# Two edits to the second block of a two-block network: the latents' norms summed on TensorE, and the last feed-forward's first four column tiles computed ahead of its norm's factor

## Chip, cores and metric

The kernel runs as one program on one core of a Trainium2 chip. The metric is the device time of one execution in microseconds, as a median over runs. All numbers of the profile come from one profiled execution of the kernel before.

## The reference, cut to what matters

A first block (two transformer layers over 256 tokens of width 1024) makes `h`, whose last step is `rmsnorm(h, final_norm)`. That result is the stream `x` of a second block, which normalises it again, modulates it, mixes it in several branches, and closes with a feed-forward. `D` is 1024, the feed-forward's width is 2816, and tokens are held in a permuted order that changes nothing here.

```
x  = rmsnorm(h, final_norm)                               # end of block one
hn = rmsnorm(x, norm1_g) * (1 + sc1) + sh1                # both factors: the "latents' two norms"
mix = ... dn_inputs, recurrence, branches of hn ...
x  = x + g1 * mix
a, b = split((rmsnorm(x, norm2_g) * (1 + sc2) + sh2) @ w_ffn_in)
x  = x + g2 * ((silu(a) * b) @ w_ffn_out)                 # the last feed-forward
return rmsnorm(x, final_g)
```

With `r` the factor of a token (a number per column of the transposed layout, where features lie on partitions and tokens on the free axis), `(x * gain * r + sh) @ W = r * ((x * gain) @ W) + sh @ W`. The first product needs no `r`, and `sh @ W` is one number per output feature.

## The kernel before

All activations are transposed: `[128 partitions, 8, 256]`, feature on partition and block, token on the free axis. Every large product is exact to float32 by three fp32r matmuls (`mm3`, L276: high weight by high x, high weight by low x, low weight by high x), all issued by `mm` at L274. A unit of weights is a `[128, 1024]` tile; `weights` (L250 to L268) loads it over SP's queue into `wst` (3 buffers), rounds it to `wh` on ScalarE in two halves (L262) and subtracts on VectorE, or on GpSimd while `onpool` is positive, to get `wl` (L263, two halves). `wh` and `wl` have 3 buffers each.

An instruction's place on its engine is not the order of the source: a planner fills each engine's queue in advance from its own costs, taking among the ready instructions the one traced first; `urgent()` moves what it holds some 100 places forward. `behind()` and `lastsq` keep weight rounding on ScalarE behind the last square. Generators run beside a main loop: `beside` and `tick` let a side generator take its next step each time a unit of weights is asked for. PSUM has two pools of 4 banks, `ps` (tiles named bank) and `acc`.

**The latents (L954 to L1006)** are a side generator beside `dn_inputs` of the context's values. `sumsq` (L301 to L324) squares the eight blocks of `h` in four ScalarE instructions of 512 columns (L309) for the first sum, and in eight of 256 columns with `final_norm` as the scale (L313) for the second; VectorE adds the four pairs (L317, L319) and folds them (L323). `col_sums` (L326) sums a `[128, 256]` tile over partitions with the tile as the stationary operand and a column of ones moving, the answer a column per 128 tokens. Four small VectorE instructions (L969 to L972) and the eight of `root` (L348 to L363) turn four columns into factors, `across` (L366, transposes at L370) spreads them over partitions as rows, and ScalarE copies the rows to `lrows` (L980, L981). Then each of the eight blocks takes two VectorE products (L988), a rounding on ScalarE (L911) and a difference on VectorE (L912). The first product of the latents that reads them is `dn_inputs` for q, whose first two units go block by block (`cols_into` with `outer`).

**The last feed-forward (L1650 to L1676)** begins where the product with `w_o` has ended. `gated_residual` (L1631) adds each block to `x2` (L1637), squares it (L1641), and adds five of the squares (L1646); four tiles of squares go to `col_sums`. `modulate` then runs `rsqrt` (L345) and `root`, `across`, and for each block the product with gain and factor (L906), rounding with the shift (L911) and difference (L912). Each `f` of 11 makes two banks `a` and `b` of two column tiles each from four units of `w_fin`; the first `f` goes block by block over two units. ScalarE takes the silu of bank a (L1668), VectorE multiplies by bank b (L1669), `split_pair` (L1410) rounds, and `down` adds the rows' product into `acc` one `f` later. `self.onpool = self.np1` (L1653) gives the first three units' differences to GpSimd.

Of the kernel before, what the change touches and what calls it, by code (L numbers as in the profile page):

```python
# [9 lines left out]
F32 = mybir.dt.float32  # L10
F32R = mybir.dt.float32r
I32 = mybir.dt.int32
AF = mybir.ActivationFunctionType
OP = mybir.AluOpType
AX = mybir.AxisListType

P = 128
T = 256
D = 1024
KD = D // P  # L20
HD = 64
EPS = 1e-6
# [6 lines left out]
NFF = 22  # L29
# [165 lines left out]
def run(g):  # L195
    for _ in g:
        pass
# [33 lines left out]
class Net:  # L231
# [722 lines left out]
    def latent(self):  # L954


        nc = self.nc
        h = self.h
        yield
        gg = self.sm.tile([P, KD], F32, name="lgg", bufs=1)  # L960
        nc.vector.tensor_mul(gg, self.gf, self.gains[:, 0])
        parts = self.lparts
        s1 = self.sumsq(h, parts=parts, eng=nc.gpsimd if 0 else nc.vector)
        s2 = self.sumsq(h, self.gf, parts=parts)
        yield
        with self.urgent():
            cs = self.col_sums((s1, s2))
            v = self.sm.tile([P, 4], F32, name="lv", bufs=1)
            nc.vector.tensor_scalar(v[:, 2:4], cs[:, 0:2], 1.0 / D, EPS, op0=OP.mult, op1=OP.add)  # L969
            nc.vector.tensor_scalar(v[:, 0:2], v[:, 2:4], D * EPS, None, op0=OP.mult)  # L970
            nc.vector.tensor_add(v[:, 0:2], v[:, 0:2], cs[:, 2:4])
            nc.vector.tensor_scalar(v[:, 0:2], v[:, 0:2], 1.0 / D, None, op0=OP.mult)  # L972
            rows = self.across(self.root(v, 4))
        yield
# [9 lines left out]
        for k in range(KD):  # L984
            q = pairs(h[:, k])
            t = self.sm.tile([P, T], F32, name="mt")
# [644 lines left out]
    def gated_residual(self, acc, gate, add):  # L1631
# [15 lines left out]
                ss[0] = s  # L1647
        return ss

    def swiglu(self):  # L1650
        nc = self.nc
        x = []
        self.onpool = self.np1  # L1653
        run(self.modulate(self.x2, self.gains[:, 2], self.mod[:, 3, 0], x, self.ss))
        pend = []

        down = self.downward(self.a["w_fout"], NFF, pend, self.ends)

        for f in range(NFF // 2):
            if f:  # L1660
                self.lastsq = None
            ab = []
            for base in (0, NFF):
                bv = self.bank2()
                self.cols_into(bv, [self.a["w_fin"][base + 2 * f + n] for n in range(2)], x, f == 0 and self.ko & 1)
                ab.append(bv)
            s = self.t2k("sw")
            nc.scalar.activation(s, ab[0], AF.Silu)  # L1668
            nc.vector.tensor_mul(s, s, ab[1])  # L1669
            ah = self.sm.tile([P, 2, T], F32R, name="ah", tag="w2k", bufs=self.nw2k)  # L1670
            al = self.sm.tile([P, 2, T], F32R, name="al", tag="w2k", bufs=self.nw2k)
            self.split_pair((ah, al), 0, s)
            pend.append((ah, al))
            if f:
                down(False)
        self.ss = self.gated_residual(down(True), self.mod[:, 5, 0], nc.gpsimd if self.gadd else nc.vector)  # L1676
# [127 lines left out]
```

## Time and profile before

| What | Value |
|---|---|
| Median of three runs | 1237.73 us |
| The three runs | 1237.47, 1237.73, 1238.69 us |
| Profiled execution, its own time | 1240.33 us |
| Its span in the trace | 1238.5 us |
| TensorE matmul busy | 1183.0 us (96%) |
| VectorE busy | 899.4 us (73%) |
| ScalarE busy | 636.3 us (51%) |
| GpSimd busy | 124.7 us (10%) |

Times in the trace are from the start of the span. PE is TensorE's matmuls, DVE VectorE, ACT ScalarE, POOL GpSimd. A busy PE is not PE at its peak, since matmuls overlap: in a full stream one of 256 columns starts every 0.12 us and is shown as 0.28 us. A float32 matmul shows as two instructions.

### The profile page before, as it was taken

To read this page: it belongs to the slowest core of one execution; us is meant where nothing else is said; L and a number is where in the kernel's file an instruction comes from. 1 tells how busy PE (TensorE), PEld (TensorE's weight loads), DVE (VectorE), ACT (ScalarE), POOL (GpSimd) and SP (SyncE) were. 2 spreads that over 40 slices of the span, in tenths; PEclk is the share of its full clock that TensorE was granted. 3 is DMA by queue.
4 is the path that set the end of the run, shared out by engine and by line. 5 is a ranking of instruction groups with operands and counts; after the bars stand their busy time and mean duration, and the time that the engine had idled before them with its cause. 6 is when DMAs were issued, how large, how long until landed. Compare 5 with 4: busy or idle time off the path is not lost.

```text
span 1238.5 us, 24745 instructions
## 1 busy us (share of the span) xinstructions
PE 1183.0 (96%) x9858; PEld 1122.1 (91%) x9858; DVE 899.4 (73%) x1784; ACT 636.3 (51%) x1247; POOL 124.7 (10%) x213
## 2 busy tenths in 40 slices
PE   8999999999999989999999799997999996999997
PEld 6779999999977889999999788897989996999997
DVE  6998996556988487675657999997665677555555
ACT  5654545555755565644445656543333545444444
POOL 1000000000010000064000310374000002000000
PEclk8999999999999989999999989998999997999998
DMA  6766687555553635457545525776423552655552
GB/s 213 238 208 240 227 291 268 185 187 188 156 174 119 210 120 173 169 171 203 164 144 165 166 83 165 240 272 215 148 81 103 179 179 86 205 187 177 186 184 85
DMA packets 65779, 221.43 MB, mean 179 GB/s; under 512 B 10048, under 2 KB 11456, under 8 KB 65664
## 3 DMA queue, kind: packets, MB, share of 16 engines
q1 hardware_dynamic: 64800, 218.29, 53.3%
q0 software_dynamic: 864, 1.57, 0.7%
q8 instruction: 77, 1.26, 0.4%
q14 instruction: 38, 0.31, 0.1%
HBM read 218.00 MB, written 1.84 MB: 177 GB/s over the span
## 4 chain that ended last, share of the span: by engine, by line
PE 64%; issue 13%; DVE 12%; POOL 6%; DMA 4%; ACT 1%; DVEq 0%; SPq 0%; POOLq 0%; ACTq 0%
PE acc L274 34%; PE bank L274 28%; DVE wl L263 3%; POOL bo L1280 1%; POOL bz L1281 1%; DVE cy L1036 1%; PE bank L565 1%; DVE xl L298 1%; DVE wmst L882 1%; DMA bl<-there 1%; DMA xc<-back 1%; ACT wh L262 1%; POOL bw L1259 1%; DMA wmst<-w_mod 1%; DVE qkT L533 1%
## 5 line engine op out<-in xcount | busy, mean ns | idle before, releaser
L262 ACT ACTIVATE wh<-wst 128x512 fp32r<-128x512 f32 x708 | 411.7, 623 | 436.8 <-PE bank L274 165.4
L263 DVE TENSOR_TENSOR wl<-wst,wh 128x512 fp32r<-128x512 f32 x696 | 464.9, 700 | 216.7 <-ACT wh L262 216.0
L274 PE MATMUL bank<-xh,wh 128*128 128x256 f32 x1024 | 293.9, 287 | 2.0 <-ACT xh L911 1.1
L274 PE MATMUL bank<-xl,wh 128*128 128x256 f32 x1024 | 293.0, 286 | 1.8 <-DVE xl L298 1.8
L274 PE MATMUL bank<-xh,wl 128*128 128x256 f32 x1024 | 292.6, 286 | 1.6 <-DVE wl L263 1.6
L274 PEld LDWEIGHTS bank<-xh,wh 128*128 128x128 f32 x1024 | 198.6, 194 | 3.2 <-ACT xh L911 1.5
L274 PEld LDWEIGHTS bank<-xh,wl 128*128 128x128 f32 x1024 | 198.6, 194 | 2.8 <-DVE wl L263 2.6
L274 PEld LDWEIGHTS bank<-xl,wh 128*128 128x128 f32 x1024 | 198.6, 194 | 2.5 <-DVE xl L298 2.4
L274 PE MATMUL acc<-ah,wh 128*128 128x256 f32 x688 | 192.1, 280 | 0.0
L274 PE MATMUL acc<-al,wh 128*128 128x256 f32 x688 | 191.7, 279 | 0.0
L274 PE MATMUL acc<-ah,wl 128*128 128x256 f32 x688 | 191.6, 279 | 0.0
L274 PE MATMUL acc<-xh,wh 128*128 128x256 f32 x640 | 184.5, 289 | 0.4 <-ACT wh L262 0.4
L274 PE MATMUL acc<-xl,wh 128*128 128x256 f32 x640 | 183.2, 287 | 0.4 <-DVE xl L912 0.4
L274 PE MATMUL acc<-xh,wl 128*128 128x256 f32 x640 | 182.8, 286 | 0.5 <-DVE wl L263 0.4
L274 PEld LDWEIGHTS acc<-ah,wl 128*128 128x128 f32 x688 | 129.2, 188 | 0.1
L274 PEld LDWEIGHTS acc<-ah,wh 128*128 128x128 f32 x688 | 129.1, 188 | 0.0
L274 PEld LDWEIGHTS acc<-al,wh 128*128 128x128 f32 x688 | 128.9, 187 | 0.0
L274 PEld LDWEIGHTS acc<-xh,wh 128*128 128x128 f32 x640 | 124.0, 194 | 2.8 <-issue 1.4
L274 PEld LDWEIGHTS acc<-xl,wh 128*128 128x128 f32 x640 | 123.9, 194 | 2.1 <-issue 1.0
L274 PEld LDWEIGHTS acc<-xh,wl 128*128 128x128 f32 x640 | 123.8, 194 | 1.3 <-DVE wl L263 0.9
L274 PE MATMUL acc<-wl,xh 128*128 128x512 f32 x176 | 70.6, 401 | 2.3 <-DVE wl L263 2.3
L274 PE MATMUL acc<-wh,xh 128*128 128x512 f32 x176 | 70.6, 405 | 1.5 <-ACT wh L262 1.5
(344 smaller groups left out, 1515.8 us busy)
## 6 DMA issues: line engine op xcount, KB each, us to landing
wst<-w_up SPq DMA_DIRECT2D x64, 512.0 KB, 3.6
wst<-w_down SPq DMA_DIRECT2D x64, 512.0 KB, 3.4
wmst<-w_mod SPq DMA_DIRECT2D x48, 512.0 KB, 4.8
wst<-w_fin SPq DMA_DIRECT2D x44, 512.0 KB, 3.3
wst<-w_in SPq DMA_DIRECT2D x39, 512.0 KB, 3.7
wst<-w_mgate SPq DMA_DIRECT2D x24, 512.0 KB, 3.3
wst<-w_fout SPq DMA_DIRECT2D x22, 512.0 KB, 3.3
wst<-w_qkv SPq DMA_DIRECT2D x20, 512.0 KB, 3.4
```

The costliest lines, as they stand in the source:

```text
L262: nc.scalar.activation(wh[:, c:c + n], st[:, c:c + n], AF.Copy)
L263: i = (nc.gpsimd if self.onpool > 0 else nc.vector).tensor_tensor(wl[:, c:c + n], st[:, c:c + n], wh[:, c:c + n].bitcast(F32), op=OP.subtract)
L274: self.nc.tensor.matmul(out, lhsT, rhs, start=start, stop=stop, skip_group_check=skip)
L298: nc.vector.scalar_tensor_tensor(xl[:, k], src, gain, xh[:, k].bitcast(F32), op0=OP.mult, op1=OP.subtract)
L533: nc.vector.tensor_copy(qk[:, :, t * P:(t + 1) * P], bk.rearrange("p (c q) -> p c q", c=4))
L565: nc.tensor.transpose(bk[:, c * P:(c + 1) * P], s[:, g, c * P:(c + 1) * P], self.ident)
L882: nc.vector.scalar_tensor_tensor(pr, st, 1.0, cv[v], op0=OP.mult, op1=OP.mult, accum_out=mod[:, part, v, k:k + 1])
L1036: nc.vector.scalar_tensor_tensor(y4[:, j], pad[:, j, :, tap:tap + CHUNK], w[:, j, tap:tap + 1], y4[:, j], op0=OP.mult, op1=OP.add)
L1259: pool.tensor_tensor(w, A[t][:, a].rearrange("p h (b j) -> p h b j", b=4), m, op=OP.mult)
L1280: pool.tensor_tensor(o, lt[:, c:, j:c].to_broadcast([P, n, c]), Z[:, j:c, 0:c].to_broadcast([P, n, c]), op=OP.mult)
L1281: pool.tensor_tensor(Z[:, c:, 0:c], Z[:, c:, 0:c], o, op=OP.subtract)
```

## The change

The latents' sums go to TensorE: each pair of squared blocks is the stationary operand, and two columns move, one of ones and one of the squares of `final_norm`, so that both sums come of one set of squares. The squares scaled by `final_norm` and VectorE's additions are gone.

In the last feed-forward, `ahead` rounds `x2 * gain` (no factor, no shift) to a pair `U` with two more columns, the shift and zero. `ahead_units` traces the norm's sum and `root`, then the products of `U` with the first two units (tiles 0 and 1 of a), then the row and the modulated pair `x` for all later `f`, then tiles 0 and 1 of b from `U`. Each of the four tiles fills one bank of 258 columns; column 256 is the shift's product, which is copied out and added as ScalarE's bias or in a VectorE product after the row's factor. The line that gave three units' differences to GpSimd is gone.

```diff
--- before.py
+++ after.py
@@ -959,16 +959,24 @@
         yield
         gg = self.sm.tile([P, KD], F32, name="lgg", bufs=1)
         nc.vector.tensor_mul(gg, self.gf, self.gains[:, 0])
-        parts = self.lparts
-        s1 = self.sumsq(h, parts=parts, eng=nc.gpsimd if 0 else nc.vector)
-        s2 = self.sumsq(h, self.gf, parts=parts)
-        yield
+        w2 = self.sm.tile([P, KD, 2], F32, name="lw2", bufs=1)
+        nc.vector.memset(w2[:, :, 0:1], 1.0)
+        nc.vector.tensor_mul(w2[:, :, 1:2], self.gf[:, :, None], self.gf[:, :, None])
+        cs = self.bank()[:, 0:4].rearrange("p (t c) -> p t c", t=2)
+        for j in range(4):
+            sq = self.t2k("sq")
+            nc.scalar.activation(sq, h[:, 2 * j:2 * j + 2], AF.Square)
+            for n in range(2):
+                k = 2 * j + n
+                for t in range(2):
+                    self.mm(cs[:, t], sq[:, n, t * P:(t + 1) * P], w2[:, k], k == 0 and t == 0, k == KD - 1, True)
+            if j == 2:
+                yield
         with self.urgent():
-            cs = self.col_sums((s1, s2))
             v = self.sm.tile([P, 4], F32, name="lv", bufs=1)
-            nc.vector.tensor_scalar(v[:, 2:4], cs[:, 0:2], 1.0 / D, EPS, op0=OP.mult, op1=OP.add)
+            nc.vector.tensor_scalar(v[:, 2:4], cs[:, :, 0], 1.0 / D, EPS, op0=OP.mult, op1=OP.add)
             nc.vector.tensor_scalar(v[:, 0:2], v[:, 2:4], D * EPS, None, op0=OP.mult)
-            nc.vector.tensor_add(v[:, 0:2], v[:, 0:2], cs[:, 2:4])
+            nc.vector.tensor_add(v[:, 0:2], v[:, 0:2], cs[:, :, 1])
             nc.vector.tensor_scalar(v[:, 0:2], v[:, 0:2], 1.0 / D, None, op0=OP.mult)
             rows = self.across(self.root(v, 4))
         yield
@@ -1647,26 +1655,77 @@
                 ss[0] = s
         return ss
 
+    def ahead(self):
+
+
+        nc = self.nc
+        U = [self.act.tile([P, KD, T + 2], F32R, name=n, tag="xs", bufs=4) for n in ("uh", "ul")]
+        sh = self.sm.tile([P, KD, 2], F32, name="ush", bufs=1)
+        nc.vector.memset(sh[:, :, 1:2], 0.0)
+        nc.vector.tensor_copy(sh[:, :, 0:1], self.mod[:, 3, 0][:, :, None])
+        nc.scalar.activation(U[0][:, :, T:], sh, AF.Copy)
+        nc.vector.tensor_sub(U[1][:, :, T:], sh, U[0][:, :, T:].bitcast(F32))
+        for k in range(KD):
+            self.split(self.x2[:, k], k, self.gains[:, 2, k:k + 1], U[0][:, :, 0:T], U[1][:, :, 0:T])
+        self.xs = x = self.pair()
+        return U, x
+
+    def ahead_units(self, U):
+        nc = self.nc
+        r = []
+        steps = self.row_steps(self.x2, r, ss=self.ss)
+        next(steps)
+        next(steps)
+        bv, row = [], None
+        for base in (0, NFF):
+            w = [self.weights(self.a["w_fin"][base + n]) for n in range(2)]
+            bk = [self.bank() for _ in range(2)]
+            for k in range(KD):
+                for n in range(2):
+                    ws = slice(k * P, k * P + P)
+                    self.mm3(bk[n][:, 0:T + 2], (w[n][0][:, ws], w[n][1][:, ws]), (U[0][:, k], U[1][:, k]), k == 0, k == KD - 1)
+            bv += bk
+            if row is None:
+                run(steps)
+                row = self.sm.tile([P, T], F32, name="nrow")
+                nc.scalar.activation(row, r[0], AF.Copy)
+                for k in range(KD):
+                    self.modulated(self.x2, k, self.gains[:, 2], self.mod[:, 3, 0], row, *self.xs)
+        c = self.sm.tile([P, 4], F32, name="usc", bufs=1)
+        s, t = self.t2k("sw"), self.t2k("sq")
+        for i, b in enumerate(bv):
+            n = i % 2
+            nc.vector.tensor_copy(c[:, i:i + 1], b[:, T:T + 1])
+            nc.vector.tensor_mul(t[:, n], b[:, 0:T], row)
+            if i < 2:
+                nc.scalar.activation(s[:, n], t[:, n], AF.Silu, bias=c[:, i:i + 1])
+                if n == 1:
+                    t = self.t2k("sq")
+            else:
+                nc.vector.scalar_tensor_tensor(s[:, n], t[:, n], c[:, i:i + 1], s[:, n], op0=OP.add, op1=OP.mult)
+        return s
+
     def swiglu(self):
         nc = self.nc
-        x = []
-        self.onpool = self.np1
-        run(self.modulate(self.x2, self.gains[:, 2], self.mod[:, 3, 0], x, self.ss))
         pend = []
+        U, x = self.ahead()
 
         down = self.downward(self.a["w_fout"], NFF, pend, self.ends)
 
         for f in range(NFF // 2):
             if f:
                 self.lastsq = None
-            ab = []
-            for base in (0, NFF):
-                bv = self.bank2()
-                self.cols_into(bv, [self.a["w_fin"][base + 2 * f + n] for n in range(2)], x, f == 0 and self.ko & 1)
-                ab.append(bv)
-            s = self.t2k("sw")
-            nc.scalar.activation(s, ab[0], AF.Silu)
-            nc.vector.tensor_mul(s, s, ab[1])
+            if f == 0:
+                s = self.ahead_units(U)
+            else:
+                ab = []
+                for base in (0, NFF):
+                    bv = self.bank2()
+                    self.cols_into(bv, [self.a["w_fin"][base + 2 * f + n] for n in range(2)], x)
+                    ab.append(bv)
+                s = self.t2k("sw")
+                nc.scalar.activation(s, ab[0], AF.Silu)
+                nc.vector.tensor_mul(s, s, ab[1])
             ah = self.sm.tile([P, 2, T], F32R, name="ah", tag="w2k", bufs=self.nw2k)
             al = self.sm.tile([P, 2, T], F32R, name="al", tag="w2k", bufs=self.nw2k)
             self.split_pair((ah, al), 0, s)
```

## Rows read from the trace of the kernel before

**Rows 1.** Page, parts 1 and 5: busy; group, count, busy us, mean ns, idle.

```profile
PE 1183.0 (96%) x9858; PEld 1122.1 (91%) x9858; DVE 899.4 (73%) x1784; ACT 636.3 (51%) x1247; POOL 124.7 (10%) x213
...
L262 ACT ACTIVATE wh<-wst 128x512 fp32r<-128x512 f32 x708 | 411.7, 623 | 436.8 <-PE bank L274 165.4
```

**Rows 2.** TensorE's waits: us in total, times, longest.

```profile
PE bank L370 <- DVE rsy L361: 17.1, 4, 7.6
...
PE bank L274 <- DVE U L1309: 6.7, 1, 6.7
```

**Rows 3.** Windows, latents: length, busy us of PE, PEld, DVE, ACT, POOL, clock, DMA.

```profile
691.00:703.60 12.60, 12.52 (x105) 12.29 (x103) 11.83 (x23) 11.34 (x24) 3.98 (x8) 1.00 0.59 174
703.60:714.50 10.90, 3.19 (x14) 2.14 (x12) 9.08 (x22) 5.01 (x15) 8.74 (x18) 0.71 0.45 146
714.50:718.30 3.80, 3.75 (x17) 3.40 (x18) 3.80 (x10) 2.54 (x7) 1.97 (x4) 0.50 0.00 0
718.30:724.20 5.90, 5.90 (x51) 5.51 (x49) 5.90 (x20) 2.80 (x6) 0.15 (x2) 0.99 0.00 0
...
735.00:760.00 25.00, 24.11 (x249) 21.71 (x248) 24.83 (x55) 9.89 (x20) 1.93 (x6) 1.00 0.47 148
```

**Rows 4.** Groups of VectorE, 691 to 727 us: count, busy us, mean ns, idle.

```profile
L319 DVE TENSOR_TENSOR ssp<-ssp,sq 128x512 f32<-128x512 f32 x4 | 2.7, 685 | 0.0
...
L317 DVE TENSOR_TENSOR ssp<-sq 128x512 f32<-128x512 f32 x2 | 1.4, 682 | 0.0
...
L970 DVE TENSOR_SCALAR lv<-lv 128x2 f32<-128x2 f32 x1 | 1.2, 1221 | 0.0
L323 DVE TENSOR_TENSOR ss<-ssp 128x256 f32<-128x256 f32 x2 | 0.8, 414 | 0.0
```

**Rows 5.** VectorE's timeline, latents: start, us, instruction.

```profile
700.90 0.41 DVE L323 TENSOR_TENSOR ss<-ssp 128x256 f32<-128x256 f32 x1
...
702.66 0.15 DVE L969 TENSOR_SCALAR lv<-bank 128x2 f32<-128x2 f32 x1
...
709.01 1.31 DVE L361 SCALAR_TENSOR_TENSOR rsy<-rst,rsy 128x4 f32<-128x4 f32 x1
```

**Rows 6.** ScalarE's timeline, latents: the scaled squares, first four.

```profile
695.25 1.70 ACT L313 ACTIVATE sq<-h,k_final_norm 128x256 f32<-128x256 f32 x4
```

**Rows 7.** GpSimd's timeline, latents and feed-forward.

```profile
700.99 5.52 POOL L263 TENSOR_TENSOR wl<-wst,wh 128x512 fp32r<-128x512 f32 x4
...
1025.65 7.38 POOL L263 TENSOR_TENSOR wl<-wst,wh 128x512 fp32r<-128x512 f32 x6 [171.35 <-ACT wh L262]
```

**Rows 8.** TensorE's timeline, start of the feed-forward.

```profile
1024.34 1.57 PE L274 MATMUL bank<-ones,sq 128*128 128x1 f32 x12
```

**Rows 9.** Windows of the feed-forward's start, columns as in rows 3.

```profile
1035.20:1039.20 4.00, 3.90 (x18) 3.88 (x19) 3.55 (x9) 2.11 (x6) 0.00 (x0) 0.50 0.13 49
...
1044.50:1050.10 5.60, 5.60 (x46) 5.60 (x47) 1.98 (x4) 3.25 (x6) 0.00 (x0) 1.00 0.47 148
```

**Rows 10.** Groups of VectorE, 1019 to 1050 us, columns as in rows 4.

```profile
L1637 DVE SCALAR_TENSOR_TENSOR x<-acc,hg,x 128x256 f32<-128x256 f32 x8 | 3.6, 476 | 2.5 <-PE acc L274 2.5
L912 DVE SCALAR_TENSOR_TENSOR xl<-mt,mod,xh 128x256 fp32r<-128x256 f32 x8 | 3.5, 483 | 0.7 <-ACT xh L911 0.7
L906 DVE SCALAR_TENSOR_TENSOR mt<-x,gains,bank 128x256 f32<-128x256 f32 x8 | 3.5, 475 | 0.8 <-PE bank L370 0.8
L263 DVE TENSOR_TENSOR wl<-wst,wh 128x512 fp32r<-128x512 f32 x4 | 2.6, 689 | 3.7 <-ACT wh L262 3.7
L1646 DVE TENSOR_TENSOR ss<-ss,sq 128x256 f32<-128x256 f32 x3 | 1.2, 417 | 0.1
L355 DVE TENSOR_TENSOR rst<-rsy 128x2 f32<-128x2 f32 x1 | 1.2, 1193 | 0.0
```

**Rows 11.** VectorE's timeline, the same chain at the end of the kernel.

```profile
1229.81 0.16 DVE L345 TENSOR_SCALAR rsv<-bank 128x2 f32<-128x2 f32 x1 [1.32 <-PE bank L274]
...
1231.38 0.16 DVE L361 SCALAR_TENSOR_TENSOR rsy<-rst,rsy 128x2 f32<-128x2 f32 x1
```

## The prediction

> **What bounds the kernel now.** I read the page first: TensorE's matmuls are busy 1183.0 of 1238.5 us, VectorE 899.4 [rows 1], so the kernel is a nearly full TensorE stream with a few holes, and an edit pays where it closes a hole. TensorE's waits name them: 17.1 us in four waits for the last instruction of `root`, the longest 7.6 us, and one wait of 6.7 us late in the mixer for `U` of the recurrence [rows 2]. Two of the four are where this change works: the latents' norms, and the last feed-forward's norm.
>
> The windows show the first place [rows 3]. From 691 to 703.6 us TensorE (12.52 of 12.60) and VectorE (11.83) are both full. From 703.6 to 714.5 us TensorE works 3.19 of 10.9 us: the context's values are done and the latents are not ready. Its granted clock falls with that idleness, and is 0.50, the lower level of 1.2 GHz, until 718.3 us. VectorE is full again at 714.5 to 718.3 us and at 735 to 760 us (24.83 of 25), so in the mixer it stands close behind TensorE as a bound.
>
> At the second place the sum over partitions ends at 1024.34 + 1.57 = 1025.9 us [rows 8], `root` waits and works until 1033.5 us, and the first 18 matmuls from 1035.2 us run at 0.50 of the clock, 3.9 us for what takes 18 x 0.12 = 2.2 us at full clock; from 1044.5 us the stream is full, and 46 matmuls end the first `f` at 1050.1 us [rows 9]. After that nothing but TensorE counts until the tail.
>
> **Why `root` is slow there.** Its small instructions take 1.19 us [rows 10] while GpSimd subtracts for three units from 1025.65 to 1033.0 us [rows 7]. At the end of the kernel, with GpSimd idle, the same nine take 1229.81 to 1231.54, 1.73 us [rows 11]. In the latents L970 (1.22 us) and L361 (1.31 us) are stretched in the same way [rows 4, 5], inside GpSimd's stretch from 700.99 us on [rows 7].
>
> **The latents, step by step.** Removed from VectorE: 2.7 + 1.4 + 0.8 = 4.9 us by durations [rows 4]; some 0.6 us of that is overlap of neighbouring records, so 4.3; two tiny instructions for the columns are added at about 0.15 each, as L969 [rows 5]. Net 4.0 us. Removed from ScalarE: eight squares, 2 x 1.70 = 3.4 us [rows 6], off the path itself but ahead of the second sum. Added to TensorE: 16 products, two instructions each, against eight removed. Twelve one-column instructions take 1.57 us [rows 8], 0.131 each; a second column is taken as free, since 128 stationary columns are loaded for each. (32 - 8) x 0.131 = 3.1 us more. It falls into the full stretch before 703.6 us and moves the values' end to 706.7 us; what hides it is the hole, which lasts past the end of `root` at 710.3 us [rows 5], and if that hole closes it costs its 3.1 us.
>
> The chain: the last plain square ends by about 695.3 us (the scaled ones follow at 695.25 [rows 6]). Its eight instructions take 1.05 us, with 0.3 us of hand-over L969 starts at 696.7 instead of 702.66 us [rows 5]: 6.0 us earlier. From there the twelve small instructions, the spreading and the eight blocks are the same work. If the chain decides, 6.0 us are won, and up to 1.7 us more from a clock that need not fall (17 matmuls in 3.75 us [rows 3] against 2.0). If VectorE's queue decides, only what is taken off it, 4.0 us. VectorE is full on both sides of the hole, so I lean to it: 5 us. The ends: 7.7 us, and 0 if the mixer is held elsewhere.
>
> **The feed-forward, step by step.** The products of tiles 0 and 1 of a (48 matmuls) no longer need the row. They need `U`, block by block, and the differences of units 0 and 1, which are now VectorE's. From 1025.9 us VectorE has at most: `root` 1.7 us [rows 11], eight differences for `U` at 0.48, 3.9 us, priced as L912, and four halves at 0.69, 2.8 us [rows 10]: 8.4 us, to 1034.3 us. (Part of `U` will be done sooner: before 1025.9 us VectorE has 3.6 us of L1637 and four L1646 at 0.42.) The second unit's first half is the last that block 0 needs, so the stream starts between 1030 and 1033 us; I take 1031.5. TensorE has by then stood nearly still for 5 us, so I take the half clock for 18 matmuls again, 1.7 us: 1031.5 + 5.8 + 1.7 = 1039.0.
>
> Then tiles 0 and 1 of b. Unit 3 can be rounded only when the first units' buffers are free, at the end of that: 0.62 us on ScalarE [rows 1] and 0.69 on VectorE [rows 10], 1.3 us in which TensorE waits as it does now. 1039.0 + 1.3 + 5.8 = 1046.1 us for the first matmul of the next `f`, against 1050.1: 4 us won. VectorE's check: 1034.3 + 3.5 + 3.5 (L906, L912) + 2.8 for units 2 and 3 + 0.6 for reading the first bank (0.15 and 0.48) = 1044.7 us, just under 1046.1. So VectorE is all but the bound, and its queue is where it can go wrong. Ends: 7 us (start at 1030.3, full clock, 1.3 of waiting: 1043.2) and 1.5 us (unit 3's half behind the modulated blocks, near 1041.5, and 5.8 after it, with queueing).
>
> **Small edits.** Two more columns in 96 matmuls are 192 columns, under 0.1 us at the 0.12 us for 256. The shift's four tiny instructions need only the modulation and fit before the stage. Two silu of half the size replace one: at most 0.5 us on ScalarE, which is idle there. The closing of the first `f` grows on VectorE from one product to four columns, four products and two more, some 3.5 us; behind it in VectorE's queue stand the halves of units 4 and 5, and TensorE waits for those. No DMA is added; unit 3's load, on SP's queue behind the release of unit 0's buffer, starts later than now, and unit 3's wait for the end of the first 48 matmuls covers it. If that cover is gone, the load shows in full.
>
> **Sum.** 5 + 4 = 9 us. The profiled execution took 1240.33 us (span 1238.5) and would take 1231.3; it stands 2.6 above the median, so in medians 1237.73 - 9 = **1228.7 us**.
>
> **Rivals.**
> *The mixer is held elsewhere.* For it: VectorE full at 735 to 760 us and a 6.7 us wait behind the recurrence's chain [rows 2, 3]. Against: those chains also begin with the latents. Only the feed-forward counts: 1233.7 us. Chance 0.15.
> *GpSimd gets in the earlier chain's way.* ScalarE has less to do and could round q's units sooner, so GpSimd's four halves move along with the chain. Six of its instructions would take 1.19 instead of 0.16 us, where two do now: 4 x 1.03 = 4.1 us back. 0.9 + 4 = 4.9 us: 1232.8 us. Chance 0.15. The Trainium skill has a rule for it (SBUF — State Buffer, Who interferes with whom): a VectorE instruction with two inputs in SBUF waits out a whole GpSimd instruction that reads SBUF. The stretched rows agree in that they are stretched; L970 has one input and is stretched too [rows 4].
> *VectorE becomes the bound of the feed-forward* (the slower side). All four `ps` banks are held by the first `f`, where two were, so the next `f` waits for VectorE to read one. If its queue runs in series, modulated blocks and both last units first (1034.3 + 7.0 + 2.8 = 1044.1), the products of b end at 1049.9, closing (some 2.9) and unit 4's half (0.7) follow, 1053.5, and the half clock costs 1.7 again: 1055.2, 5 us later than now. With the latents at their low end of 0: 1242.8 us. It decides from the point where the next `f` starts later than 1050.1 us by more than the latents gave. Chance 0.1.
> *The order does not change.* The planner could keep the products behind the row, or spend the gain in another order of the mixer: 1237.7 us. Chance 0.05.
>
> **How the numbers follow.** The forecast has the other 0.55, with 1224.5 to 1232.5 for itself. A measurement here tells 0.2%, 2.5 us, from no change, so faster is under 1235.2. Faster: 0.55 and nearly all of the first two rivals and the edges of others, 0.79; same 0.11; slower 0.10. The range goes up over the first two rivals to the unchanged time, 1238, and down to both terms at their upper ends, 1237.7 - 14.7 = 1223, with 2 us for planner order: 1221.
>
> **What would show it.** Right: no wait of TensorE over 3 us for `root` in the latents, L969 near 697 us and the first product of q before 709 us; no GpSimd work at the feed-forward's start, `root` near 2 us, matmuls from `U` before 1033 us, the next `f` some 4 us sooner after the end of `w_o`'s products. Wrong: the next `f` waiting for VectorE's differences or for a bank; small instructions of over 1 us in the latents' chain; a hole later in the mixer that has grown by what was won.

## The result, and the profile after

| | before | after |
|---|---|---|
| Median, same chip, 4 runs each | 1238.21 us (1237.47 to 1238.85) | 1224.53 us (1222.64 to 1229.78) |
| Ratio, 95% interval | | 0.9895 [0.9873, 0.9918] |
| Profiled execution, its own time | 1240.33 us | 1224.34 us |
| Its span | 1238.5 us | 1222.2 us |

The change wins 13.7 us between the medians; the forecast was 9, and the time lies inside the range. But the gain did not come from where the sum put it. Two instructions cut each trace in three: the last addition to `h` at the end of the two layers, and the first `x` of the closing feed-forward. The views by line, VectorE's instructions, give them (count, shortest, median and longest ns, first and last start). Of the kernel before:

```profile
L784 DVE TENSOR_TENSOR h<-h,gt x8: 673/682/692, 326.4 to 694.0; 128x512 f32<-128x512 f32 x8
...
L1637 DVE SCALAR_TENSOR_TENSOR x<-acc,hg,x x8: 472/476/484, 1019.3 to 1024.1; 128x256 f32<-128x256 f32 x8
```

Of the changed kernel:

```profile
L784 DVE TENSOR_TENSOR h<-h,gt x8: 682/684/693, 322.8 to 687.2; 128x512 f32<-128x512 f32 x8
...
L1645 DVE SCALAR_TENSOR_TENSOR x<-acc,hg,x x8: 475/478/485, 1009.2 to 1014.3; 128x256 f32<-128x256 f32 x8
```

The layers end 6.8 us earlier (694.0 to 687.2), and nothing of the change stands there. The mixer, from there to the first `x`, takes 322.0 us instead of 325.3. The feed-forward, from the first `x` to the end of the span, takes 213.0 instead of 219.2. So 6.8 us have no place in the prediction, and the latents' 5 us are at most 3.3. A kernel that is the one before with nothing but larger tiles (pad2, below) shows 322.3 and 216.2 us in these two parts, so some 3 us of either gain are not the edits' work.

The page and TensorE's waits (us in total, times, longest) of the changed kernel, for [rows 1, 2]:

```profile
PE 1174.3 (96%) x9882; PEld 1111.4 (91%) x9882; DVE 899.3 (74%) x1804; ACT 635.6 (52%) x1250; POOL 119.9 (10%) x207
```

```profile
PE bank L274 <- DVE U L1317: 5.4, 1, 5.4
PE bank L274 <- DVE wl L263: 3.4, 7, 0.6
...
PE bank L370 <- DVE rsy L361: 3.1, 2, 1.9
PE bank L1143 <- DVE tokk L1134: 2.8, 1, 2.8
...
PE acc L274 <- ACT xh L911: 2.2, 2, 1.3
```

The waits for `root` fell from 17.1 to 3.1 us, as hoped (1.1 us more, of the latents' transposes, is put down to `hb`, a tiny instruction right behind `root`), and the long one in the mixer for `U` from 6.7 to 5.4. New are waits for `tokk` and, in `acc`, for `xh`. The windows of the latents show what became of the hole (columns as in [rows 3]):

```profile
697.00:702.00 5.00, 4.64 (x40) 4.40 (x38) 4.24 (x7) 2.34 (x7) 2.99 (x3) 1.00 0.33 110
702.00:707.00 5.00, 2.36 (x14) 1.88 (x14) 5.00 (x9) 2.53 (x6) 5.00 (x10) 0.93 0.00 0
707.00:712.00 5.00, 4.23 (x20) 3.67 (x21) 4.92 (x16) 4.75 (x11) 1.66 (x10) 0.50 0.31 105
```

TensorE no longer stands still behind `root`; it starves later, 2.36 of 5 us from 702 us on, with VectorE and GpSimd both full (5.00 and 5.00), and then runs at 0.50 of the clock, the 1.2 GHz level, as it did before. The chain itself came early. VectorE's timeline, for [rows 5], and ScalarE's:

```profile
691.82 0.16 DVE L977 TENSOR_SCALAR lv<-bank 128x2 f32<-128x2 f32 x1 [3.11 <-PE bank L274]
...
696.02 0.16 DVE L361 SCALAR_TENSOR_TENSOR rsy<-rst,rsy 128x4 f32<-128x4 f32 x1
...
700.55 2.76 DVE L996 SCALAR_TENSOR_TENSOR mt<-h,lgg,lrows 128x128 f32<-128x128 f32 x4
```

```profile
700.26 0.26 ACT L988 ACTIVATE lrows<-bank 128x128 f32<-128x128 f32 x1
```

Counted from the last `h`, `root` begins its last step after 8.8 us (15.0 before), but the rows are copied 4.2 us behind it (2.6 before), and four products `mt` take 2.76 us (1.54 before), beside GpSimd. L977 brings a wait that was not there: VectorE stands 3.11 us for TensorE's column sums, with halves of the next units behind it in its queue.

The feed-forward's start, for [rows 8, 11]; first TensorE:

```profile
1014.91 1.55 PE L274 MATMUL bank<-ones,sq 128*128 128x1 f32 x12
...
1016.77 0.48 PE L274 MATMUL bank<-uh,wh 128*128 128x258 f32 x1 [0.31 <-ACT wh L262]
...
1032.78 0.28 PE L274 MATMUL bank<-xh,wh 128*128 128x256 f32 x1
...
1036.11 0.38 PE L274 MATMUL bank<-xh,wl 128*128 128x256 f32 x1 [0.59 <-DVE wl L263]
```

Then VectorE:

```profile
1016.50 0.16 DVE L345 TENSOR_SCALAR rsv<-bank 128x2 f32<-128x2 f32 x1 [0.53 <-PE bank L274]
...
1021.06 0.15 DVE L361 SCALAR_TENSOR_TENSOR rsy<-rst,rsy 128x2 f32<-128x2 f32 x1
```

The matmuls on `uh` begin 0.3 us after the sum's end. The first matmul of the next `f` comes 23.6 us after the first `x` (1032.78 - 1009.2), 30.8 before (1050.1 - 1019.3): 7.2 us won, of which 6.2 reach the end. The windows there, for [rows 9]:

```profile
1016.50:1023.60 7.10, 5.91 (x24) 5.32 (x25) 5.92 (x19) 2.82 (x6) 0.00 (x0) 0.53 0.32 95
1023.60:1032.70 9.10, 9.10 (x76) 8.96 (x75) 8.14 (x21) 7.38 (x15) 0.00 (x0) 0.99 0.41 156
1032.70:1040.00 7.30, 6.52 (x51) 5.95 (x50) 6.37 (x15) 3.98 (x9) 0.00 (x0) 1.00 0.34 106
```

The half clock (0.53) is spent on products that before could not have run at all; from 1023.6 us the stream is full; from 1032.7 us TensorE misses 0.8 us, waiting among others for VectorE's halves. GpSimd does nothing.

One execution of a kernel differs from the next by up to some 7 us here (after: 1222.64 to 1229.78), so below ratios decide how much, and traces how.

### The profile page after: what moved, and what is told of

Same layout as the page of the kernel before. It is cut to its first block, busy times and chain, and to the rows that moved or that the text cites. A ratio compares the mean times of both kernels' runs of the same rounds, so it can differ in the third digit from the quotient of the medians.

```text
span 1222.2 us, 24807 instructions
## 1 busy us (share of the span) xinstructions
PE 1174.3 (96%) x9882; PEld 1111.4 (91%) x9882; DVE 899.3 (74%) x1804; ACT 635.6 (52%) x1250; POOL 119.9 (10%) x207
## 4 chain that ended last, share of the span: by engine, by line
PE 72%; DVE 13%; DMA 6%; POOL 4%; issue 3%; ACT 2%; SPq 0%; DVEq 0%; POOLq 0%; ACTq 0%
PE acc L274 38%; PE bank L274 33%; DVE wl L263 4%; DMA wmst<-w_mod 2%; DVE xl L298 1%; POOL bo L1288 1%; POOL bz L1289 1%; ACT wh L262 1%; DVE wmst L882 1%; PE bank L565 1%; DVE h L704 1%; DVE cy L1044 1%; DMA back<-bzt 1%; DVE qkT L533 1%; DMA pt<-pT 0%
## 5 line engine op out<-in xcount | busy, mean ns | idle before, releaser
L263 DVE TENSOR_TENSOR wl<-wst,wh 128x512 fp32r<-128x512 f32 x702 | 470.1, 703 | 208.5 <-ACT wh L262 208.0
L274 PE MATMUL bank<-xl,wh 128*128 128x256 f32 x992 | 280.5, 283 | 2.1 <-DVE xl L298 2.1
L274 PE MATMUL bank<-xh,wl 128*128 128x256 f32 x992 | 279.4, 282 | 2.9 <-DVE wl L263 2.9
L274 PE MATMUL bank<-xh,wh 128*128 128x256 f32 x992 | 281.3, 284 | 0.8 <-ACT wh L262 0.8
L274 PE MATMUL acc<-al,wh 128*128 128x256 f32 x688 | 191.6, 279 | 0.0
L274 PE MATMUL acc<-ah,wl 128*128 128x256 f32 x688 | 191.3, 279 | 0.0
L274 PE MATMUL acc<-ah,wh 128*128 128x256 f32 x688 | 191.2, 279 | 0.0
L274 PEld LDWEIGHTS bank<-xh,wl 128*128 128x128 f32 x992 | 187.0, 189 | 4.3 <-DVE wl L263 4.3
L274 PEld LDWEIGHTS bank<-xl,wh 128*128 128x128 f32 x992 | 187.0, 189 | 2.8 <-DVE xl L298 2.7
L274 PEld LDWEIGHTS bank<-xh,wh 128*128 128x128 f32 x992 | 187.1, 189 | 1.6 <-ACT wh L262 1.2
L274 PE MATMUL acc<-xh,wh 128*128 128x256 f32 x640 | 183.4, 287 | 2.2 <-ACT xh L911 2.2
L274 PE MATMUL acc<-xl,wh 128*128 128x256 f32 x640 | 182.0, 285 | 1.5 <-DVE xl L912 1.5
L274 PE MATMUL acc<-xh,wl 128*128 128x256 f32 x640 | 181.1, 284 | 0.5 <-DVE wl L263 0.4
L274 PEld LDWEIGHTS acc<-al,wh 128*128 128x128 f32 x688 | 129.0, 188 | 0.0
L274 PEld LDWEIGHTS acc<-ah,wl 128*128 128x128 f32 x688 | 128.9, 188 | 0.1
L274 PEld LDWEIGHTS acc<-ah,wh 128*128 128x128 f32 x688 | 128.9, 188 | 0.0
L274 PEld LDWEIGHTS acc<-xh,wh 128*128 128x128 f32 x640 | 121.6, 190 | 4.7 <-ACT xh L911 2.8
L274 PEld LDWEIGHTS acc<-xl,wh 128*128 128x128 f32 x640 | 121.5, 190 | 2.9 <-DVE xl L912 1.7
L274 PEld LDWEIGHTS acc<-xh,wl 128*128 128x128 f32 x640 | 121.9, 191 | 1.5 <-DVE wl L263 0.9
L274 PE MATMUL acc<-wl,xh 128*128 128x512 f32 x176 | 70.6, 401 | 2.5 <-DVE wl L263 2.4
L274 PE MATMUL acc<-wh,xh 128*128 128x512 f32 x176 | 70.8, 406 | 1.1 <-ACT wh L262 1.1
```

Source lines behind the costliest of these rows:

```text
L263: i = (nc.gpsimd if self.onpool > 0 else nc.vector).tensor_tensor(wl[:, c:c + n], st[:, c:c + n], wh[:, c:c + n].bitcast(F32), op=OP.subtract)
L274: self.nc.tensor.matmul(out, lhsT, rhs, start=start, stop=stop, skip_group_check=skip)
```

## The experiments

Each kernel was timed beside the kernel before on the same chip.

| Run | What it is | Median us | Ratio to before |
|---|---|---|---|
| lat | latents' edit alone | 1238.84 | 1.0007 [0.9995, 1.0019] |
| ffn | feed-forward's edit alone | 1225.67 | 0.9902 [0.9881, 0.9923] |
| pad2 | before, big slots 64 bytes wider | 1231.36 | 0.9941 [0.9921, 0.9960] |
| nocol | after, big slots as before | 1232.04 | 0.9957 [0.9944, 0.9970] |
| pad4 | before, big slots 128 bytes wider | 1234.93 | 0.9975 [0.9964, 0.9986] |
| shift | before, only the 2 KB tiles moved | 1237.45 | 0.9991 [0.9982, 1.0000] |
| pad2_dve | pad2, no GpSimd at the feed-forward | 1226.98 | 0.9917 [0.9897, 0.9938] |
| lat_rows | lat, rows copied at once | 1239.56 | 1.0013 [1.0003, 1.0022] |
| lat_np0 | lat, no GpSimd halves for q | 1234.95 | 0.9980 [0.9970, 0.9990] |
| before_np0 | before, no GpSimd halves for q | 1235.23 | 0.9978 [0.9967, 0.9990] |
| lat_conv | lat, context's values first | 1236.84 | 0.9994 [0.9983, 1.0004] |
| after_np0 | after, no GpSimd halves for q | 1221.29 | 0.9864 [0.9847, 0.9881] |

### The parts, and where the tiles lie

The two columns of `U` make its tiles 8 x 258 x 4 = 8256 bytes a partition instead of 8192. They share four slots with every large input of the kernel (`xs`: `xh`, `xl` of all stages), so all four slots move apart by 64 bytes, and all that is allocated behind them moves too. The theory was that this makes TensorE's stream faster everywhere; the rival that the 6.8 us are scatter between executions.

**lat** has the change's first hunk alone (the squares and column sums in `latent`):

```
-        s1 = self.sumsq(h, parts=parts, eng=nc.gpsimd if 0 else nc.vector)
-        s2 = self.sumsq(h, self.gf, parts=parts)
...
+                    self.mm(cs[:, t], sq[:, n, t * P:(t + 1) * P], w2[:, k], k == 0 and t == 0, k == KD - 1, True)
```

> The latents' edit alone, xs slots 8192 bytes apart as before. Theory P: 3 to 4 us faster than the kernel before, near 1234.5, the start of the latents where it was (h last added near 694 us). Rival N: more, 6 to 10 us, since then all that was ahead at the mixer's end was this edit's or scatter.

**ffn** has the other hunk alone (`ahead`, `ahead_units`, and in `swiglu`):

```
-        self.onpool = self.np1
-        run(self.modulate(self.x2, self.gains[:, 2], self.mod[:, 3, 0], x, self.ss))
...
+        U, x = self.ahead()
```

> The feed-forward's edit alone, with the wider xs slots that it brings. Theory P: 6 us by placement and 6 by the feed-forward's start: near 1226. Rival N: 6 us in all, near 1232, and h last added at 694 us.

**pad2** is the kernel before with one tile of that kind declared wider; the instructions and their order are the same on every engine, only four additions to it see two rows of 256 instead of 512 in a row.

```
-        g0 = self.act.tile([P, KD, T], F32, name="g0", tag="xs", bufs=4)
+        g0 = self.act.tile([P, KD, T + 2], F32, name="g0", tag="xs", bufs=4)[:, :, 0:T]
```

> The kernel before with one tile of the xs tag (g0) declared two columns wider, so that the four xs slots lie 8256 bytes apart as in the changed kernel, and all that follows them moves too; no instruction is added or removed. Theory P (the part of the gain that lies ahead of both edits comes from where the tiles lie): about 6 us faster than the kernel before, near 1232, with 48 matmuls of the first layer's stream in 5.65 us instead of 5.76, and the last block of h added near 687 us instead of 694. Rival N (it is scatter between executions): within 2 us of the kernel before, streams at 5.76.

**nocol** is the changed kernel with `U` of T columns, so that the slots stay where they were. It leaves out the product of the weights with the shift in the first `f`, and copies a column of the tokens' product in its place.

```
-        U = [self.act.tile([P, KD, T + 2], F32R, name=n, tag="xs", bufs=4) for n in ("uh", "ul")]
+        U = [self.act.tile([P, KD, T], F32R, name=n, tag="xs", bufs=4) for n in ("uh", "ul")]
...
-                    self.mm3(bk[n][:, 0:T + 2], (w[n][0][:, ws], w[n][1][:, ws]), (U[0][:, k], U[1][:, k]), k == 0, k == KD - 1)
+                    self.mm3(bk[n][:, 0:T], (w[n][0][:, ws], w[n][1][:, ws]), (U[0][:, k], U[1][:, k]), k == 0, k == KD - 1)
```

> Both edits, but U without its two columns, so that the xs slots lie 8192 bytes apart as before. It leaves out the shift's product (a column of the token's product is copied and added in its place), the count of instructions is the same but for three tiny ones. Theory P: 6 us slower than the changed kernel, near 1230.5. Rival N: the same as the changed kernel, near 1224.5.

Measured: the slots alone give 0.59% (7.3 us), the feed-forward's edit 0.39% on top of them (0.9902 against 0.9941), and in the old slots both edits together give 0.43%. The latents' edit gives nothing that can be measured (1.0007). It is placement, not scatter: pad2's interval ends at 0.996, and executions of the same mean granted clock, 0.979, took 1231.1 to 1233.4 us in pad2 and 1239.6 to 1240.2 in the kernel before. The shapes of TensorE's line L274 (ns shortest, median, longest) show it too. Before, pad2 and after:

```profile
L274 PE MATMUL bank<-xh,wh x1024: 277/283/579, 120.2 to 1215.5; 128*128 128x256 f32 x171
...
L274 PE MATMUL acc<-xh,wh x640: 278/283/583, 91.1 to 1023.0; 128*128 128x256 f32 x160
```

```profile
L274 PE MATMUL bank<-xh,wh x1024: 274/279/580, 119.1 to 1202.4; 128*128 128x256 f32 x171
...
L274 PE MATMUL acc<-xh,wh x640: 274/281/581, 90.5 to 1012.6; 128*128 128x256 f32 x160
```

```profile
L274 PE MATMUL bank<-xh,wh x992: 274/281/562, 120.2 to 1199.2; 128*128 128x256 f32 x199
```

With three shapes each, 3 x (1024 + 640) = 4992 matmuls read the big slots. If each comes 2 ns sooner, that is 10 us (an estimate); so a few ns are enough for the 7.3.

Two more runs ask whether the slots' distance counts or where each tile lies. **pad4** has `T + 4` in the same line, **shift** moves the 2 KB tiles (`ah`, `al`, squares) and what lies behind them by 256 bytes, as far as four slots of 64 bytes more push them, and leaves the slots 8192 apart:

```
-        m = self.sm.tile([P, 2], F32, name="smax")
+        m = self.sm.tile([P, 34], F32, name="smax")[:, 0:2]
```

> The kernel before with its four big input slots 8320 bytes apart (8192 before, 8256 in the earlier run that gave 1231.36): the same instructions in the same order on every engine as that run, only addresses differ. Theory P2 (a distance that is a multiple of 8192, or the place of the tiles to each other, slows TensorE's stream): any other distance does as well, the 48 matmuls of the first layer's stream take 5.65 us and the time is 1230 to 1233. Rival (it is where each tile lies, finer than that): the stream's pace differs from both, 5.65 to 5.8 us, and the time lies anywhere from 1231 to 1240.

> The kernel before with one small tile ahead of the 2 KB tiles made 128 bytes wider per buffer, so that the 2 KB tiles (ah, al, squares, norms) and all behind them lie 256 bytes further, as in the changed kernel, while the four big input slots stay 8192 bytes apart: the same instructions in the same order. Theory D (the distance of the big slots counts): nothing changes, 1237 to 1239.5, the matmuls on xh and xl take 283 ns in the first layer as before. Theory S (each operand's own place counts): the matmuls on ah and al, 279 to 280 ns before, take 276 to 277 as in the changed kernel, those on xh and xl stay at 283, and the time falls by a part of the 7 us, to 1232 to 1236.

In shift the shapes are as before. In pad4 the median falls by 1 ns for `xl` (283 before) and not for `xh`:

```profile
L274 PE MATMUL bank<-xh,wh x1024: 277/283/579, 119.9 to 1212.7; 128*128 128x256 f32 x171
```

```profile
L274 PE MATMUL bank<-xh,wh x1024: 274/284/580, 119.3 to 1206.3; 128*128 128x256 f32 x171
L274 PE MATMUL bank<-xl,wh x1024: 275/282/583, 120.2 to 1206.4; 128*128 128x256 f32 x171
```

So the place of the 2 KB tiles is not it (0.9991), the slots' is. Other distances than 8192 do not do equally well: 8320 gives 0.25%, 8256 gives 0.59%. Why is open; no run tells which operands have to lie how.

### Why the latents' edit gives nothing

In lat the hole behind `root` is gone as in the changed kernel, and L977 runs at 698.74 us (702.66 before). Three theories: the rows wait in ScalarE's queue (Q), GpSimd's halves eat the gain (G), or the mixer is held by something else (E).

**lat_rows** puts the copies of the rows inside the urgent block, right behind `across`:

```
             rows = self.across(self.root(v, 4))
+            rs = self.t2k("lrows")
...
+                nc.scalar.activation(two(rs[:, i, 0:P]), q[0], AF.Copy)
```

> The latents' edit alone (1238.84 us, ratio 1.0007 to before) with the four copies of the norm's rows (lrows) put right behind the rows' transposes in ScalarE's queue, ahead of the next unit's cth. In the trace of the latents' edit alone the rows are across at 704.1 us and copied only at 708.6 to 709.3, because ScalarE first waits 2.85 us for cy, which waits for GpSimd's copies of pad. Theory Q (the gain is lost in that queue): the copies start by 704.5, the first mt by 705 (708.9 without), TensorE's waits for xh and xl (3.5 us together) are gone, and the time falls by 2 to 4 us to 1235 to 1237, ratio 0.997 to 0.9985. Theory E (the mixer is held elsewhere, by VectorE from 735 on): the copies come early just the same and the time stays within 1 us of 1238.8, ratio 1.000 to 1.0015.

Q falls. ScalarE of lat, then of lat_rows:

```profile
707.52 0.63 ACT L1082 ACTIVATE cth<-cy 128x512 f32<-128x512 f32 x1 [2.85 <-DVE cy L1044]
...
708.58 0.26 ACT L988 ACTIVATE lrows<-bank 128x128 f32<-128x128 f32 x1
...
710.72 0.51 ACT L911 ACTIVATE xh<-mt,mod 128x256 fp32r<-128x256 f32 x1 [0.86 <-DVE mt L996]
```

```profile
702.84 0.28 ACT L987 ACTIVATE lrows<-bank 128x128 f32<-128x128 f32 x1 [0.29 <-PE bank L370]
...
704.19 0.55 ACT L911 ACTIVATE xh<-mt,mod 128x256 fp32r<-128x256 f32 x1
```

The latents' first block is rounded from 704.19 us on, 11.4 us after `h` (18.5 before, at 712.54), and the ratio is 1.0013.

**lat_np0** and **before_np0** take the three units behind the layers, whose differences GpSimd makes, back to VectorE:

```
-        self.np2 = 3
+        self.np2 = 0
```

> The latents' edit alone with the three weight units after the first layers that take their difference on GpSimd (six instructions, 1.3 to 2.5 us each there) taking it on VectorE (0.69 us each, 4.1 us in all). Theory G (GpSimd's differences beside VectorE's and ahead of the copies of pad cost the edit its gain: vj stretched to 1.43 us, mt to 0.68, cy waiting 2.6): stretched rows between 700 and 726 fall back to 0.4 and 0.28, the waits for xh, xl and vj (5 us) shrink, and the time falls by 2 to 4 us to 1235 to 1237. Theory E (held by VectorE later, which is 95% busy from 735 to 840): 4 us more of VectorE's work ahead of it gives no gain, 1238 to 1241.

> The kernel before, its latents' norms as they were, with the same three weight units taking their difference on VectorE as in the run lat_np0 (ratio 0.998, 1234.95 us). It tells whose gain that was. If GpSimd was what ate the latents' gain, it gives nothing where the sum still ends late: 1237 to 1240, ratio 0.999 to 1.002. If GpSimd's halves cost the mixer the same whichever norm stands ahead of them, it falls as lat did, by 2 to 4 us to 1234 to 1236, ratio 0.997 to 0.9985, and the latents' edit is worth nothing without GpSimd either.

Both win the same, 0.9980 and 0.9978. GpSimd's halves do cost some 3 us there, but not on account of the edit: without them too the edit is worth nothing. What they cost shows on VectorE's products `vj` of the context's values (view by line, ns shortest, median, longest). Of lat, then lat_np0:

```profile
L1084 DVE SCALAR_TENSOR_TENSOR vj<-cth,cy x8: 417/422/1479, 708.2 to 784.0; 128x256 f32<-128x256 f32 x8
```

```profile
L1084 DVE SCALAR_TENSOR_TENSOR vj<-cth,cy x8: 408/418/425, 704.5 to 775.1; 128x256 f32<-128x256 f32 x8
```

The longest stand beside GpSimd's halves, as VectorE's and GpSimd's timelines of lat show:

```profile
722.47 2.86 DVE L1084 SCALAR_TENSOR_TENSOR vj<-cth,cy 128x256 f32<-128x256 f32 x2
```

```profile
719.95 5.09 POOL L263 TENSOR_TENSOR wl<-wst,wh 128x512 fp32r<-128x512 f32 x2 [3.33 <-ACT wh L262]
```

By the Trainium skill (SBUF — State Buffer, Who interferes with whom) VectorE and GpSimd lock one shared pair of SBUF ports; the rows agree: 1479 ns beside GpSimd, 425 at most without.

That leaves E. The mixer's steps, from the traces (us; "scan" is the first product of `dv` and `tokk` on TensorE, "U" VectorE's first `U` of the long wait):

| Kernel | last h | h to scan | scan to U | h to first x |
|---|---|---|---|---|
| before | 694.0 | 33.9 | 133.5 | 325.3 |
| lat | 694.1 | 36.7 | 131.5 | 326.1 |
| lat_rows | 692.8 | 37.8 | 130.7 | 326.3 |
| lat_conv | 693.4 | 33.6 | 131.4 | 323.9 |
| before_np0 | 694.7 | 31.1 | 130.6 | 320.4 |
| lat_np0 | 692.0 | 28.5 | 132.6 | 318.8 |
| shift | 692.4 | 33.8 | 130.6 | 323.4 |
| nocol | 692.3 | 36.0 | 130.2 | 324.5 |
| pad2 | 686.6 | 33.8 | 130.8 | 322.3 |
| after | 687.2 | 33.8 | 131.4 | 322.0 |

(A trace is one execution: lat's took 1241.29 us, the slowest of its runs, lat_np0's 1231.96, the fastest. So the steps count here, not the spans.) From the scan to `U` every kernel takes 130.2 to 133.5 us, wherever the latents are. Some 3 us of that are scatter: shift has the same instructions as the kernel before, and takes 130.6 where that takes 133.5. When the scan over the context begins scatters far less, 33.7 to 34.1 us after `h` in the six traces that have neither the latents' edit nor `np2 = 0`, and that scan needs the context's values (`cy`, `vj`), not the norms. **lat_conv** puts these first in the queues:

```
+                up = self.urgent() if name == "v" and ctx else ExitStack()
+                up.__enter__()
                 y = self.conv(bv, self.k["dn_conv"][:, c:c + 2], ctx)
...
+                up.__exit__(None, None, None)
```

> The latents' edit alone (1238.84 us, ratio 1.0007) with the context's last value columns (the convolution cy and its product vj) put ahead of the latents' mt and xl in the engines' queues. In the traces so far the scan over the context begins (the first 16 products of dv and tokk on TensorE) 33.9 us after h's last instruction in the kernel before and 36.7 with the latents' edit alone, and 131.5 to 133.5 us pass from there to U in either, and 130.6 to 132.6 in five others. Theory C (the mixer ends by the context's chain, which starts with vj and knows nothing of the norms; latents that come earlier only stand in its way): the scan begins 28 to 34 us after h, 3 to 8 earlier than in the edit alone, and the time falls by 2 to 5 us to 1234 to 1237, ratio 0.996 to 0.9990. Rival (what x brings, q and k of the latents, ends last): the scan begins earlier, the chain behind it is longer by as much, and the time stays at 1238 to 1240.

The scan's first products in lat, then in lat_conv:

```profile
730.82 1.16 PE L274 MATMUL bank<-dv,tokk 64*128 64x128 f32 x16
```

```profile
726.98 1.16 PE L274 MATMUL bank<-dv,tokk 64*128 64x128 f32 x16
```

Counted from `h`, the scan begins 3.1 us earlier than in lat; that the order in the queues does this is shown, by one trace of each. That the time follows is not: `U` comes 3.1 us earlier as well, but that is no more than the scatter above, the medians differ by 2.0 us, the ratio 0.9994 misses the expected 0.9990, and the intervals of the two runs overlap (lat's from 0.9995, lat_conv's to 1.0004).

The order is not all that delays lat's scan (33.9 to 36.7). TensorE's windows of lat, then of the changed kernel (columns as in [rows 3]), cover the stream behind the latents' column sums:

```profile
694.10:698.90 4.80, 4.80 (x45) 4.80 (x44) 1.62 (x4) 2.42 (x5) 0.00 (x0) 1.00 0.54 157
698.90:702.30 3.40, 3.40 (x19) 3.40 (x18) 2.95 (x16) 0.00 (x0) 0.00 (x0) 0.51 0.47 152
```

```profile
692.00:694.50 2.50, 2.50 (x24) 2.50 (x23) 2.31 (x11) 0.51 (x1) 0.00 (x0) 1.00 0.37 131
```

In lat the granted clock falls to the 1.2 GHz level though TensorE was busy all the time before, with the 32 two-column instructions of the sums among its matmuls; 3.4 us at 0.51 cost 1.7 us (an estimate). The five traces that have this edit in the old slots all show the fall (lat, lat_rows, lat_conv, lat_np0, nocol), the two in the wide slots (after, after_np0) do not, and in the changed kernel the scan begins 33.8 us after `h`, as before. Why is open. lat and lat_conv both have the fall, so it does not explain the 3.1 us between them.

So in the changed kernel the earlier norms cost the scan nothing, and still win nothing: pad2 without the edit takes 322.3 us from `h` to the first `x`, the changed kernel 322.0. `U` itself does come of the latents, not of the scan: it is made from their keys (`kT`) by way of a matrix inverse on GpSimd and a DMA into `xc`. VectorE's last keys of the kernel before and its step before `U`, then the last keys of lat:

```profile
765.37 0.75 DVE L1076 SCALAR_TENSOR_TENSOR kT<-cth,cy 128x256 f32<-128x256 f32 x2
...
860.79 0.76 DVE L1309 TENSOR_TENSOR Tm<-xc,k_d_blk 128x256 f32<-128x256 f32 x2 [8.24 <-DMA xc<-back]
```

```profile
767.01 0.75 DVE L1084 SCALAR_TENSOR_TENSOR kT<-cth,cy 128x256 f32<-128x256 f32 x2
```

Counted from `h`, the last keys come after 71.4 us before, 72.9 in lat, 74.0 in lat_rows and 70.1 in the changed kernel, although the first block is there after 18.5, 16.6, 11.4 and 15.2 us. Between 730 us and the keys, VectorE is busy 35.5 of 35.9 us in the kernel before and 37.0 of 37.5 in lat, TensorE 34.8 and 36.5: the keys wait their turn among the scan's products and the weights' halves. Without GpSimd's halves they come after 68.6 us (before_np0) and 69.2 (lat_np0). So the mixer is held behind the norms, E. That VectorE's queue is what holds the keys is argued from these rows; no run tests it.

### What the feed-forward's gain is made of

**pad2_dve** is pad2 with nothing computed ahead, only GpSimd out of the way:

```
-        self.np1 = 3
+        self.np1 = 0
```

> The kernel before with the wider slots (1231.36 us) and without GpSimd's differences at the start of the feed-forward: VectorE takes the three units' six halves, the norm's root and the 2 x 8 instructions of the modulated input, nothing is computed ahead. If most of what the feed-forward's edit brought (5 to 6 us) is that GpSimd is out of the root's way, the root falls from 7.5 us to below 2.5, and the time to 1226 to 1228. If it is the computing ahead, the root falls too, but VectorE has six halves of 0.68 us (4.1 us) more among the inputs, TensorE still starves until the first ones, and the time is 1229 to 1233.

VectorE's `root` in pad2, then in pad2_dve:

```profile
1015.47 0.16 DVE L345 TENSOR_SCALAR rsv<-bank 128x2 f32<-128x2 f32 x1 [1.25 <-PE bank L274]
...
1016.59 1.19 DVE L355 TENSOR_TENSOR rst<-rsy 128x2 f32<-128x2 f32 x1
...
1022.89 0.16 DVE L361 SCALAR_TENSOR_TENSOR rsy<-rst,rsy 128x2 f32<-128x2 f32 x1
```

```profile
1015.41 0.16 DVE L345 TENSOR_SCALAR rsv<-bank 128x2 f32<-128x2 f32 x1 [1.25 <-PE bank L274]
...
1015.81 0.16 DVE L355 TENSOR_TENSOR rst<-rsy 128x2 f32<-128x2 f32 x1
...
1019.86 0.15 DVE L361 SCALAR_TENSOR_TENSOR rsy<-rst,rsy 128x2 f32<-128x2 f32 x1
```

`root` falls from 7.6 us to 4.6, not below 2.5, since VectorE's own halves now stand between its steps; the expectation's size for it was wrong, its time (1226.98) was right. By the medians GpSimd out of the way is worth 0.24%, 3.0 us, and the computing ahead the rest, 0.15% (0.9917 to 0.9902). Neither step alone stands clear of its interval; that the edit as a whole wins is clear in the old slots (nocol, 0.9957, against lat, 1.0007).

The traces show both steps. From the first `x` to the first matmul of the next `f`, pad2 takes 30.3 us, pad2_dve 27.9 and the changed kernel 23.6; from the first `x` to the end they take 216.2, 214.2 and 213.0 (ffn 213.2). So the computing ahead brings the next `f` 4.3 us forward, and 1.2 us of that reach the end. About half of what is lost goes to a slower stream. ScalarE's silu of the changed kernel's ten later `f`, then the first of the same ten in pad2_dve, whose last starts at 1195.3 us:

```profile
L1727 ACT ACTIVATE sw<-bank x10: 577/579/579, 1040.5 to 1194.5; 128x512 f32<-128x512 f32 x10
```

```profile
1042.90 0.58 ACT L1668 ACTIVATE sw<-bank 128x512 f32<-128x512 f32 x1
```

Nine steps of the same work take 154.0 us there and 152.4 here. `U` takes two of the four slots, so the inputs of the later `f` may lie in others than in pad2_dve; that this is the reason is not tested.

### The changed kernel without GpSimd's halves behind the layers

**after_np0** is the changed kernel with the line of before_np0, `self.np2 = 0`:

> The changed kernel (1224.53 us, ratio 0.9895) with those three units' differences on VectorE. If GpSimd's price is one for the place between the layers and the mixer, the gain of lat_np0 over lat (0.9980 against 1.0007, 3 us) adds up with the other parts: 1220.5 to 1222.5, ratio 0.986 to 0.988. If it was the one trace's luck, 1223 to 1226.

The parts add: 1221.29 us, ratio 0.9864. Against the changed kernel that is 3.2 us between the medians, as much as before_np0 and lat_np0 won; the two intervals (to 0.9881, from 0.9873) overlap a little. The scan begins 26.8 us after `h`, the earliest of all, and the keys come after 67.5.

## Why the prediction was right, and where it was not

- **The number** was right by luck, by errors that cancel in part: 5 us for the latents that are not there, 7 us of placement that the sum did not have, and a feed-forward that was 1 us too low.
- **The latents: the step failed.** The chain did move: L977 runs 4.6 us after `h` where L969 ran 8.7 after it (4.0 won, 6.0 forecast), `root`'s last step comes 6.2 us earlier, and the hole behind it is gone. The steps that fail are "if the chain decides, 6.0 us are won" and its lower half, the 4.0 us taken off VectorE's queue: VectorE now stands 3.11 us at L977, and the last keys come 1.3 us earlier, not 4 to 6. The rival that the mixer is held elsewhere was right. The argument against it, that "those chains also begin with the latents", is true of the data, but an earlier start was not an earlier end: keys 70 to 74 us behind `h`, wherever the norms were. Its price, 1233.7 us, is about what the two edits give in the old slots: nocol 1232.04.
- **GpSimd in the earlier chain's way** was right that its halves move along and stretch VectorE, wrong in what they stretch: of the small instructions one, L360 (1.23 us; the others 0.15 to 0.17 in the changed kernel), but above all `vj`, and `mt`, which stands beside GpSimd's halves and its own product of `h`. It costs as much without the change.
- **The feed-forward: right that the next `f` comes sooner, too low.** 4 us were forecast for the next `f`; it came 7.2 sooner, 2.4 of them by GpSimd's absence alone (pad2 to pad2_dve) and 0.5 by placement alone (30.8 to 30.3). In the time the parts give 4.8 (ffn over pad2) to 5.3 (nocol). Matmuls on `uh` started 7.6 us after the first `x`, where 12.2 (1031.5) was forecast: ScalarE and VectorE had rounded part of `U` during the residual, and TensorE began with the blocks that were ready, at half clock. `root` took 4.7 us, not 1.7, but nobody waited for it. VectorE did not become the bound. What the sum lacked is what is given back behind the start of the next `f`: 3.1 us against pad2_dve, of which 1.6 is the slower stream; the rest includes waits for VectorE's halves.
- **What was left out:** a tile made 64 bytes wider moves the other tiles of its pool. The text priced the two columns at under 0.1 us of TensorE and said nothing of their place.

## What to carry to other kernels

Before a hole is closed, follow the work behind it to the end of the stage: if it has to pass an engine that is full anyway, an earlier start need not be an earlier end. When an edit changes a tile's size, time the old kernel with the new size alone, or its gain is credited to the wrong part. Work given to GpSimd to relieve VectorE is worth a run without it: taking it back won about 3 us behind the layers, shown by two runs, and by one run's median as much at the feed-forward.

## What the runs showed of the hardware that was not expected

The pace of a stream of equal matmuls depended on where its operands lay: with the big slots 8192, 8256 and 8320 bytes apart, with the same instructions in the same order, the kernel took 1238, 1231.4 and 1234.9 us, and the median matmul on `xh` 283, 279 and 284 ns (on `xl` 283, 280 and 282). The medians do not rank the three as the times do, so they do not explain them alone.

TensorE's granted clock fell to its lower level (0.51 in lat) in the middle of a full stream, behind 32 two-column instructions, in all five traces that have them in the old slots, and in neither of the two in the wide slots.
